# Mixture of experts: weights as one stream, bias products behind the previous gemm, and three smaller edits

## The chip, the cores and the metric

The kernel runs on one core of a Trainium2 chip. The metric is the device time of one execution in microseconds (us), the median of several runs. The engines of the core work in parallel, each with a queue of its own that is worked off in order: TensorE (PE for its products, PEld for its weight loads), VectorE (DVE), ScalarE (ACT), GpSimd (POOL) and SyncE (SP, which issues most DMAs here). An instruction at the head of a queue that waits for a semaphore holds up all that stands behind it on that engine.

## The reference, cut to what matters

Three transformer blocks in sequence, 512 tokens of 1024 features. The change lies in the second half of the first block, a mixture of 32 experts of which each token takes four (two small edits lie in block 1's start and in block 2):

```python
def moe(h, w_router, b_router, w1, b1, w2, b2):       # 512 x 1024
    logits = xf @ w_router + b_router
    top_val, top_idx = lax.top_k(logits, 4)
    gates = jax.nn.softmax(top_val, axis=-1)
    ...                                                # tokens sorted by expert
        u = xb @ w1[e] + b1[e]                         # 1024 -> 2048
        glu = jnp.minimum(u[:, ::2], 7.0)
        lin = jnp.clip(u[:, 1::2], -7.0, 7.0)
        a = glu * jax.nn.sigmoid(1.702 * glu) * (lin + 1.0)
        return a @ w2[e] + b2[e]                       # 1024 -> 1024
    ...                                                # y[token] += gate * result
```

Block 2 is an attention with a scalar `lam`, worked out from four vectors of 64 (`lambda_vecs`), and other mixers.

## The kernel before, in words

`moe` (L933) first ranks the experts by how many tokens they have, on the chip: expert 0 stands at position 0, the others at positions 1 to 31 by falling count. Each position has a block of fixed room: 128 tokens for positions 0 to 5, 96 for 6 to 9, 80 for 10 to 16, 64 for 17 to 31; positions 1 and 2 have a second block of 64 ("heavy"). Positions 3 to 16 are called large, 17 to 31 small. What doesn't fit goes to overflow blocks in a loop at the end (L1416), which runs zero times with these inputs. The order in which the experts are worked is 0, 3, 17, 4, 5, 18, 6, 7, 19, ... : mostly two large ones and a small one, with a heavy one in between and three small ones behind it; the last one is small.

Each expert has three gemms of eight k-tiles: two halves of w1 and then w2. Its weights come in 12 loads of 1 MB on SP's queue (`wload`, L944), into nine buffers `mraw` and two `raw`, one load for two k-tiles. In position order 0 to 16 each k-tile of weights is split into two numbers of reduced precision: ACT writes hi (L302), and DVE lo = raw - hi (L303; POOL for a few tiles of expert 0). The tiles whi/wlo have three buffers, a pair `ws` is used for every fourth. A large expert takes per k-tile six products of 512 columns (hi by x hi, hi by x lo, lo by x hi, two halves each), a small one two, with the raw weights (L1269). The products of one gemm add up in a PSUM bank; large ones alternate between mm0 and mm1, small ones between s0 and s1. Each gemm begins with the bias, itself a product (L1252 for a small block, L1255 for a large one), which opens the bank.

After a w1 half the epilogue reads the bank: DVE gl (L1283), ACT gt (L1284), DVE ln (L1285), DVE twice (L1286, L1287), then PE transposes gl (L1212), and ACT and DVE put the result down as the operand of w2 (L1204, L1206). After w2, `scatter` (L1328) weighs the rows by their gates on ACT (yr, L1330 or L1333) and POOL adds them to `yd` in DRAM by an indirect DMA. Slots without a token are added to 128 extra rows of yd (`dump`).

The tokens of a block come by an indirect DMA of POOL from `hrow`, the normalized tokens in DRAM (L1222, L1226), and are transposed on PE (L1212). For expert 0, four products of 0/1 matrices A0 with the token numbers (L1064) give the list gi. Its first four k-tiles are split ahead (L1180 to L1182): three behind `last`, the operation that writes gi, the fourth with its lo on POOL. The tables of all other blocks (`tables`, L1087, and `tables2`, L1161) are worked out during expert 0.

The order of the instructions in each engine's queue isn't the order of the program alone: a planner draws it up ahead of time, by program order as priority, with costs of its own for every operation and by when it thinks that the operands are there. `tc.issue_after(x)` holds what is inside it behind x on the same engine.

`block2` loads the four vectors (lv, L1515) on POOL's queue and works out the lambdas with a few small operations of DVE and ACT (to L1526).

Of the kernel before, what the change touches and what calls it, by code (L numbers as in the profile page):

```python
# [11 lines left out]
F32 = mybir.dt.float32  # L12
# [10 lines left out]
T = 512  # L23
# [511 lines left out]

def block1_mixer(k):
# [18 lines left out]
    cs = k.silu_col(k.v("c"))  # L555
    b = k.v("b_ada")
# [341 lines left out]
def moe_rows(k):  # L898

    nc = k.nc  # L900
    ps = k.pt("t")[0:8, 0:128]
    nc.tensor.transpose(ps, k.mod1[:, 24:32], k.ident)
    t = k.sm.tile([128, T], F32, tag="tmp", name="sh", bufs=3)
    nc.scalar.activation(t[0:8, 0:128], ps, AF.Copy)
    shd = k.dr.tile([1, D], F32, name="shd")
    nc.gpsimd.dma_start(shd.rearrange("o (n c) -> (o n) c", c=128), t[0:8, 0:128])
    k.hrow = k.dr.tile([T, D], F32, name="hrow")
    nc.gpsimd.dma_start(k.hrow, shd.to_broadcast([T, D]))

    k.yd = k.dr.tile([T + 128, D], F32, name="yd")  # L910
    z = k.sm.tile([128, T], F32, tag="tmp", name="z", bufs=3)
    nc.gpsimd.memset(z, 0.0)
    for j in range(T // 128 + 1):
        nc.gpsimd.dma_start(k.yd[128 * j:128 * j + 128].rearrange("p (a f) -> p a f", a=2), z.unsqueeze(1).to_broadcast([128, 2, T]))
# [18 lines left out]
def moe(k):  # L933
# [42 lines left out]
    gi0 = mp.tile([128, 1], I32, name="gi0")  # L976
# [56 lines left out]
    dump = rp.tile([128, 2], F32, name="dump")  # L1033
    G.tensor_scalar(dump[:, 0:1], pid, T + 1.0, None, op0=ALU.add)
    G.tensor_sub(dump[:, 1:2], pid, half)
    G.tensor_scalar(dump[:, 1:2], dump[:, 1:2], 2.0 * T, None, op0=ALU.add)
# [24 lines left out]
    g0 = pg[:, 128:192]  # L1061
# [20 lines left out]
    V.tensor_tensor(sel[:, :, 0:32], rk[:, 64:96].unsqueeze(1).to_broadcast([128, 2, 32]),  # L1082
# [4 lines left out]
    def tables():  # L1087
# [64 lines left out]
        V.tensor_scalar(pad, tp3[:, 0], 0.5, dump[:, 0:1], op0=ALU.is_lt, op1=ALU.mult)  # L1152
# [4 lines left out]
        V.tensor_scalar(pad[:, c64], tab[:, 0, c64], 0.5, dump[:, 1:2], op0=ALU.is_lt, op1=ALU.mult)  # L1157
# [25 lines left out]
    nsp = [0]  # L1183

    def wsplit(raw, pool_lo, to):
# [3 lines left out]
        return k.wsplit(raw, pool_lo=pool_lo, to=to)  # L1189

# [23 lines left out]

    def gather(blocks):
# [17 lines left out]
    def expert(w1, w2, blocks, selcol, between=None, on_pool=((),) * 3, last=False, to=lambda: None):  # L1233


        X = gather(blocks)
# [7 lines left out]
        def gemm(w, ops, bcol):  # L1244

            pss = []
            for ns, *_ in blocks:
                ps = bank("s").unsqueeze(1) if ns == 64 else bank("mm", (128, 2, 512))
                o = [ps[64 * c:64 * c + 64, 0] if ns == 64 else ps[0:ns, c] for c in range(2)]
                b_ = bias[:, bcol // 2:bcol // 2 + 512]  # L1250
                if ns == 64:
                    nc.tensor.matmul(ps[:, 0], sw, b_, start=True, stop=False)  # L1252
                else:
                    for c in range(2):
                        nc.tensor.matmul(o[c], selcol[:, c].to_broadcast([128, ns]), b_, start=True, stop=False)  # L1255
                pss.append((ps, o))
            for q in range(4):
                raw = w[q]() if callable(w[q]) else w[q]
                for j in range(2):
                    kt = 2 * q + j  # L1260
                    if between and not last and bcol == 1024 and kt == 4:
                        between[0]()
                    if split:
                        hi, lo = ready.pop(0) if ready else wsplit(raw[:, j], kt in on_pool[bcol // 1024], to())
                    for op_, (_, o) in zip(ops, pss):
                        terms = ((op_[0], hi), (op_[0], lo), (op_[1], hi)) if len(op_) == 2 else ((op_[0], raw[:, j]),)
                        for n_, (l, r_) in enumerate(terms):
                            for c in range(2):
                                ins = nc.tensor.matmul(o[c], l(kt), r_[:, c * 512:(c + 1) * 512], start=False,  # L1269
                                                       stop=kt == 7 and n_ == len(terms) - 1)  # L1270
                    if kt == 3:
                        turn["half"] = ins.ins
                    for _ in range(2 if kt > 3 else 0):
                        if adds:
                            adds.pop(0)()
            return [ps if b_[0] == 64 else ps[0:b_[0]] for (ps, _), b_ in zip(pss, blocks)]
        for hf in range(2):
            for ps, (a_, _), (ns, *_) in zip(gemm([w1(hf, q) for q in range(4)], X, hf * 1024), A, blocks):
# [15 lines left out]
        pys = gemm([w2(q) for q in range(4)], [a_[1] for a_ in A], 2048)  # L1294
# [12 lines left out]
    def block(b):  # L1307
        return (ROOM + (64,) * N2)[b], tabi[:, b:b + 1] if b else gi0, tab[:, 0, b:b + 1], tab[:, 1, b:b + 1], tabi[:, b:b + 1]
# [17 lines left out]
    def scatter(py, gcol, row, ns):  # L1326

        y = pools["Y"].tile([128, D], F32, tag="Y", name="yr", bufs=1) if ns == 64 else ep.tile([128, D], F32, tag="ah", name="yr", bufs=2)  # L1328
        if ns == 64:
            S.activation(y[:, 0:512], py[:, 0], AF.Copy, scale=gcol)  # L1330
            G.indirect_dma_start(yd2, IOA(ap=row, axis=0), y[:, 0:512], None, bounds_check=2 * T + 127, compute_op=ALU.add)
# [68 lines left out]
    def first_weights():  # L1400
        w = a["w2_qk"]
        k.pre = {(id(w), u): k.wunit(w, u) for u in range(3)}
    for p in order:
        blocks = [block(p)] + ([block(31 + p)] if 1 <= p <= N2 else [])
        if p == 0:
            expert(lambda hf, q: first[4 * hf + q], lambda q: (lambda: wload(a["w2"][0, q])), blocks, sel[:, :, 0:1], (tables, tables2), ((6,), (2, 4, 6), (3,)))
            continue
        e = nc.values_load(sigi[0:1, p:p + 1], engines=(mybir.EngineType.SP,), min_val=0, max_val=31)
        own = p == order[-1]
        if own:  # L1410
            collected.extend(collect())
        expert(lambda hf, q: (lambda: wload(sq(a["w1"][bass.ds(e, 1), hf, q]), own)),
               lambda q: (lambda: wload(sq(a["w2"][bass.ds(e, 1), q]), own)), blocks, sel[:, :, p:p + 1], last=own,
               between=first_weights if own else None)
    nov = nc.values_load(ovi[0:1, 0:1], min_val=0, max_val=15)
    with tc.For_i(0, nov, 1) as i:  # L1416
# [7 lines left out]
        expert(lambda hf, q: (lambda: wload(sq(a["w1"][bass.ds(e, 1), hf, q]), True)),  # L1424
               lambda q: (lambda: wload(sq(a["w2"][bass.ds(e, 1), q]), True)), [(128, gi, gc[:, 0:1], gc[:, 1:2])], sc, last=True,
               to=lambda: [t_[:, j] for t_ in (mr.tile([128, 2, 1024], F32R, tag="mraw", name="ms", bufs=9),) for j in range(2)])
# [53 lines left out]
def block2(k):  # L1480
# [29 lines left out]
    with ExitStack() as es2:  # L1510
        p = es2.enter_context(tc.tile_pool(name="da", bufs=1))
        eb_ = p.tile([128, T], F32, name="epb")

        lv = p.tile([128, 256], F32, name="lv")
        G.dma_start(lv, a["lamv"].to_broadcast([128, 256]))  # L1515
        lt = p.tile([128, 2, 64], F32, name="lt")
        lvv = lv.rearrange("p (a b d) -> p a b d", a=2, b=2)
        V.tensor_mul(lt, lvv[:, :, 0], lvv[:, :, 1])
        lam = p.tile([128, 4], F32, name="lam")
        V.tensor_reduce(lam[:, 0:2], lt, axis=AX.X, op=ALU.add)  # L1520
        k.ln_exp(k.hi_ins)
        with tc.issue_after(k.tables.ins):
            S.activation(lam[:, 0:2], lam[:, 0:2], AF.Exp)
        V.tensor_sub(lam[:, 2:3], lam[:, 1:2], lam[:, 0:1])
        lam_init = 0.8 - 0.6 * math.exp(-0.3 * 0)
        V.tensor_scalar(lam[:, 3:4], lam[:, 2:3], -lam_init, None, op0=ALU.add)  # L1526
# [784 lines left out]
```

## Time and profile before

| | us |
|---|---|
| median of 3 runs | 3394.36 (3390.3 to 3399.63) |
| profiled execution | 3392.58 |
| its span | 3389.1, with 3.5 around it |
| PE busy in the span | 3209.7 (95%) |
| DVE, ACT, POOL busy | 1923.5, 1339.0, 415.5 |
| the experts in the span | some 711 to 1910 |

Times in the rows are us from the span's start, durations us unless ns is written. L1252 is line 1252 of the kernel. An entry [0.95 <-DVE ln L1285] says that the engine stood idle for 0.95 us before the instruction and that the end of DVE's ln released it. PEclk is the granted clock of TensorE as a share of full speed; the DMA share is the mean busy share of the core's 16 DMA engines. Products on PE are pipelined, so records of one stretch overlap.

### The profile page before, as it was taken

The numbers are of one execution on the slowest core, as the hardware profiler recorded it, in microseconds if no ns is written. First come the engines' busy times: TensorE is split into PE (matmuls) and PEld (weight loads), VectorE is DVE, ScalarE is ACT, GpSimd is POOL, SyncE is SP. The second block draws the span as 40 slices with busy tenths as digits, with TensorE's granted clock in tenths as the row PEclk, the third lists the DMA queues.
The fourth block names the chain that finished last, engine by engine and source line by source line (L and its number), as shares of the span: only waits on it lengthen the run. The fifth ranks groups of instructions, "written<-read, shape, count | busy, mean of one in ns | idle before, by whom it ended". The sixth has DMA issues, their size and how long they took to land. (4 is left out here: it accounts for less than half of the span.)

```text
span 3389.1 us, 41014 instructions
## 1 busy us (share of the span) xinstructions
PE 3209.7 (95%) x15609; PEld 2225.9 (66%) x15609; DVE 1923.5 (57%) x2927; ACT 1339.0 (40%) x1966; POOL 415.5 (12%) x519
## 2 busy tenths in 40 slices
PE   6999999979999999999998799999999999999998
PEld 5778887756755445544342377777776777678887
DVE  7651235467785567754141377766547765555655
ACT  2232344335665456543141245322235433343433
POOL 1223000131000000000100110211121011010001
PEclk9999999989999999999999899999999999999999
DMA  7437323559999999997979521454422210022222
GB/s 265 167 126 235 106 75 119 183 165 346 396 396 368 379 363 350 372 377 270 361 299 359 212 81 51 170 173 169 153 102 91 98 37 3 14 99 87 100 88 86
DMA packets 110680, 668.48 MB, mean 197 GB/s; under 512 B 14416, under 2 KB 14520, under 8 KB 42000
## 3 DMA queue, kind: packets, MB, share of 16 engines
q1 hardware_dynamic: 81952, 573.35, 44.1%
q0 software_dynamic: 28528, 92.48, 9.5%
q8 instruction: 124, 2.03, 0.2%
q14 instruction: 76, 0.62, 0.1%
HBM read 647.56 MB, written 28.63 MB: 200 GB/s over the span
## 5 line engine op out<-in xcount | busy, mean ns | idle before, releaser
L302 ACT ACTIVATE whi<-raw 128x1024 fp32r<-128x1024 f32 x354 | 373.8, 1059 | 661.1 <-PE mm L353 497.5
L303 DVE TENSOR_TENSOR wlo<-raw,whi 128x1024 fp32r<-128x1024 f32 x352 | 435.2, 1239 | 312.2 <-ACT whi L302 305.4
L352 PE MATMUL mm<-h_hi,whi 128*128 128x512 f32 x1440 | 576.7, 400 | 4.6 <-DVE th L637 1.6
L353 PE MATMUL mm<-h_lo,whi 128*128 128x512 f32 x1440 | 576.3, 400 | 0.0
L354 PE MATMUL mm<-h_hi,wlo 128*128 128x512 f32 x1440 | 575.5, 400 | 0.0
L303 DVE TENSOR_TENSOR wlo<-mraw,whi 128x1024 fp32r<-128x1024 f32 x246 | 295.3, 1218 | 75.0 <-ACT whi L302 73.0
L352 PEld LDWEIGHTS mm<-h_hi,whi 128*128 128x128 f32 x1440 | 270.8, 188 | 82.4 <-issue 12.4
L353 PEld LDWEIGHTS mm<-h_lo,whi 128*128 128x128 f32 x1440 | 271.0, 188 | 67.7 <-issue 7.0
L354 PEld LDWEIGHTS mm<-h_hi,wlo 128*128 128x128 f32 x1440 | 271.0, 188 | 67.0 <-issue 5.6
L302 ACT ACTIVATE whi<-mraw 128x1024 fp32r<-128x1024 f32 x248 | 258.6, 1056 | 92.2 <-PE mm L1269 73.7
L1269 PE MATMUL s<-mraw,x 128*64 128x512 f32 x896 | 234.8, 606 | 16.0 <-DMA mraw<-in_w_dram 15.9
L1269 PE MATMUL mm<-whi,x 128*80 128x512 f32 (+2 forms) x816 | 245.6, 405 | 2.7 <-ACT whi L302 2.7
L1283 DVE TENSOR_SCALAR gl<-s 128x256 f32<-128x256 f32 x34 | 14.4, 424 | 315.8 <-PE s L1269 315.8
L1269 PEld LDWEIGHTS mm<-whi,x 128*80 128x80 f32 (+2 forms) x816 | 135.8, 169 | 72.9 <-issue 15.7
L1269 PEld LDWEIGHTS s<-mraw,x 128*64 128x64 f32 x896 | 65.9, 138 | 140.2 <-issue 115.4
L1284 ACT ACTIVATE gt<-gl 128x256 f32<-128x256 f32 (+3 forms) x68 | 35.5, 522 | 285.8 <-DVE gl L1283 284.3
L370 PE MATMUL mm<-whi,h_hi 128*128 128x256 f32 x480 | 138.3, 288 | 3.6 <-ACT rv L589 1.9
L1269 PE MATMUL mm<-wlo,x 128*80 128x512 f32 (+2 forms) x408 | 132.8, 407 | 8.4 <-DVE wlo L303 7.2
L352 PE MATMUL mm<-fhi,whi 128*128 128x512 f32 x352 | 139.5, 396 | 0.0
L353 PE MATMUL mm<-flo,whi 128*128 128x512 f32 x352 | 139.3, 396 | 0.0
L354 PE MATMUL mm<-fhi,wlo 128*128 128x512 f32 x352 | 139.2, 395 | 0.0
L371 PE MATMUL mm<-wlo,h_hi 128*128 128x256 f32 x480 | 136.0, 283 | 2.1 <-DVE wlo L303 2.0
(733 smaller groups left out, 5546.9 us busy)
## 6 DMA issues: line engine op xcount, KB each, us to landing
mraw<-in_w_dram SPq DMA_DIRECT2D x316, 1024.0 KB, 7.8
raw<-in_w_dram SPq DMA_DIRECT2D x68, 1024.0 KB, 7.8
mw<-in_wmod_dram POOLq DMA_DIRECT2D x48, 512.0 KB, 4.3
raw<-in_w_dn_dram SPq DMA_DIRECT2D x24, 1024.0 KB, 4.8
raw<-in_w_gu_dram SPq DMA_DIRECT2D x22, 1024.0 KB, 5.6
raw<-in_w_up_dram SPq DMA_DIRECT2D x22, 1024.0 KB, 4.8
mw<-in_wada_dram POOLq DMA_DIRECT2D x32, 512.0 KB, 4.6
raw<-in_w_aqk_dram SPq DMA_DIRECT2D x12, 1024.0 KB, 4.9
```

Source lines behind the costliest of these rows:

```text
L302: nc.scalar.activation(hi, raw, AF.Copy)
L303: ins = (nc.gpsimd if pool_lo else nc.vector).tensor_sub(lo, raw, hi.bitcast(F32))
L352: nc.tensor.matmul(pss[t], hi[:, k, s], xs[0][:, k0 + k], start=first, stop=False)
L353: nc.tensor.matmul(pss[t], hi[:, k, s], xs[1][:, k0 + k], start=False, stop=False)
L354: nc.tensor.matmul(pss[t], lo[:, k, s], xs[0][:, k0 + k], start=False, stop=last)
L370: nc.tensor.matmul(ps, xs[0][:, k, s], hi[:, k % 4], start=k == 0, stop=False)
L371: nc.tensor.matmul(ps, xs[0][:, k, s], lo[:, k % 4], start=False, stop=False)
L1269: ins = nc.tensor.matmul(o[c], l(kt), r_[:, c * 512:(c + 1) * 512], start=False, stop=kt == 7 and n_ == len(terms) - 1)
L1283: V.tensor_scalar(gl, pg, 7.0, None, op0=ALU.min)
L1284: S.activation(th, gl, AF.Tanh, scale=0.5 * 1.702)
```

## The change

The weights of all experts become one `Stream` of k-tiles. After each k-tile's products it emits the splits of the next three k-tiles (the next six in a small expert), with at most three splits waiting: that is in the program before the epilogue of the gemm at hand, across gemms and experts. The first two splits of expert 0 are emitted before the router, two more behind `last`, which is now the operation that writes `sel` (L1082); POOL takes lo of the k-tiles 6, 10, 12, 14 and 19 of expert 0, as before, but no longer that of 3. The number of an expert is read by SP at its first load.

The bias products of a gemm are held behind the last weights product of the gemm before.

Expert 0's tokens are picked by products (`pick`): the four tiles of tokens stay in SBUF as rows (two in xgs, two in one mraw buffer), and 32 products of a 128x128 piece of them with A0 give x already transposed; ACT and DVE add the shift and split it. The products L1064, gi, the gather and the transposes of expert 0 fall away.

Slots without a token get an index out of bounds, which the indirect DMA skips; yd has 512 rows, and one of five DMAs that zero it falls away. The lambdas of block 2 (`lambdas`, the same operations with the product on POOL) are worked out at the start of block 1 and not at that of block 2. The loop for overflow blocks uses a stream of its own without splits ahead.

```diff
@@ in moe(), before the router
+    early = [k.wsplit(first[0][:, j]) for j in range(2)]
-    rows = [k.wp.tile([128, D], F32, tag="wlo", name="row", bufs=3) for j in range(2)]
-    for t, row in enumerate(xgs + rows):
+    rows = mr.tile([128, 2, 1024], F32, tag="mraw", name="rows", bufs=9)
+    rows = xgs + [rows[:, 0], rows[:, 1]]
+    for t, row in enumerate(rows):
@@ expert 0's places
     for t in range(4):
         V.tensor_scalar(A0[:, t], iota, p0[:, t:t + 1], M[:, 0, t:t + 1], op0=ALU.is_equal, op1=ALU.mult)
-        nc.tensor.matmul(g0, A0[:, t], tok[:, t:t + 1].to_broadcast([128, 64]), start=t == 0, stop=t == 3)
-    V.tensor_scalar(p0[:, 0:1], g0[:, 0:1], 0.5, 100000.0, op0=ALU.is_lt, op1=ALU.mult)
-    last = V.scalar_tensor_tensor(gi0, g0[:, 0:1], -1.0, p0[:, 0:1], op0=ALU.add, op1=ALU.add)
@@
-    V.tensor_tensor(sel[:, :, 0:32], rk[:, 64:96].unsqueeze(1).to_broadcast([128, 2, 32]),
+    last = V.tensor_tensor(sel[:, :, 0:32], rk[:, 64:96].unsqueeze(1).to_broadcast([128, 2, 32]),
@@ tables()
-        V.tensor_scalar(pad, tp3[:, 0], 0.5, dump[:, 0:1], op0=ALU.is_lt, op1=ALU.mult)
+        V.tensor_scalar(pad, tp3[:, 0], 0.5, 100000.0, op0=ALU.is_lt, op1=ALU.mult)
@@
-    with tc.issue_after(last.ins):
-        ready = [k.wsplit(first[j // 2][:, j % 2]) for j in range(3)]
-    ready.append(k.wsplit(first[1][:, 1], True, [ep.tile([128, D], F32R, tag=tag, name="ws", bufs=1) for tag in ("vh", "vl")]))
+    class Stream:
+        def raw(self, u):
+            while len(self.raws) <= u // 2:
+                n = len(self.raws)
+                self.raws.append(self.src[n]())
+            return self.raws[u // 2][:, u % 2]
+        def ahead(self, upto, limit=3):
+            for u in range(self.at, min(upto, len(self.big))):
+                if self.big[u] and u not in self.split:
+                    if len(self.split) >= limit:
+                        return
+                    self.split[u] = wsplit(self.raw(u), u in (6, 10, 12, 14, 19))
+        def take(self):
+            u = self.at
+            if self.big[u]:
+                self.ahead(u + 1, 99)
+            self.at += 1
+            return self.split.pop(u) if self.big[u] else self.raw(u)
...
+    def pick(At):
+        hl, at = operand("x", True, lambda v, kt: v[:, kt])
+        for n in range(8):
+            if n % 4 == 0:
+                ps = k.pt("t").rearrange("p (j s) -> p j s", s=128)
+            for t in range(4):
+                nc.tensor.matmul(ps[:, n % 4], rows[t][:, n * 128:(n + 1) * 128], At[:, t], start=t == 0, stop=t == 3)
+            sh = mod[:, 24 + n:25 + n]
+            S.activation(hl[0][:, n], ps[:, n % 4], AF.Identity, bias=sh)
+            V.scalar_tensor_tensor(hl[1][:, n], ps[:, n % 4], sh, hl[0][:, n].bitcast(F32), op0=ALU.add, op1=ALU.subtract)
+        return [at]
@@ gemm()
-            for ns, *_ in blocks:
-                ps = bank("s").unsqueeze(1) if ns == 64 else bank("mm", (128, 2, 512))
...
+            with tc.issue_after(turn["mm_ins"]) if turn.get("mm_ins") else nullcontext():
+                for ns, *_ in blocks:
...
+            for kt in range(8):
+                w = stream.take()
+                hi, lo = w if split else (None, None)
+                raw = stream.raw(stream.at - 1)
...
+                if not looped:
+                    stream.ahead(stream.at + (3 if split else 6))
+                turn["mm_ins"] = ins.ins
@@ scatter(), alike for both kinds
-            G.indirect_dma_start(yd, IOA(ap=row[0:ns], axis=0), y[0:ns], None, bounds_check=T + 127, compute_op=ALU.add)
+            G.indirect_dma_start(yd, IOA(ap=row[0:ns], axis=0), y[0:ns], None, bounds_check=T - 1, oob_is_err=False, compute_op=ALU.add)
@@ the order loop
+    for p in order:
+        stream.add(p < N1, loads(p, p == order[-1]))
+    stream.split.update(enumerate(early))
+    with tc.issue_after(last.ins):
+        stream.ahead(4, 4)
...
-            expert(lambda hf, q: first[4 * hf + q], ..., blocks, sel[:, :, 0:1], (tables, tables2), ((6,), (2, 4, 6), (3,)))
+            expert(blocks, sel[:, :, 0:1], pick(A0), (tables, tables2))
```

## Rows read from the trace of the kernel before

**Rows 1.** the page, part 1: busy us (share of the span) x instructions, by engine.

```profile
PE 3209.7 (95%) x15609; PEld 2225.9 (66%) x15609; DVE 1923.5 (57%) x2927; ACT 1339.0 (40%) x1966; POOL 415.5 (12%) x519
```

**Rows 2.** waits of PE, 780 to 1860 us: who, for whom, us in total, times, longest.

```profile
PE s L1252 <- DVE ln L1285: 19.8, 21, 1.0
PE s L1252 <- ACT yr L1330: 8.7, 11, 0.8
PE mm L1255 <- ACT yr L1333: 8.6, 11, 0.9
PE mm L1269 <- DVE wlo L303: 7.6, 28, 0.6
PE mm L1269 <- ACT whi L302: 2.7, 6, 0.4
```

**Rows 3.** stretches: us, busy us (x) of PE, PEld, DVE, ACT, POOL, PEclk, DMA share, GB/s.

```profile
1237.20:1267.10 29.90, 26.76 (x113) 8.68 (x113) 4.11 (x11) 4.50 (x10) 4.07 (x5) 1.00 1.00 386
1160.20:1267.10 106.90, 100.39 (x439) 53.96 (x439) 71.40 (x81) 58.51 (x69) 7.96 (x8) 1.00 0.97 371
1140.00:1160.00 20.00, 18.02 (x78) 5.87 (x76) 2.49 (x6) 3.44 (x7) 1.61 (x3) 1.00 1.01 418
1622.00:1707.00 85.00, 79.65 (x338) 26.56 (x336) 10.93 (x26) 10.88 (x23) 13.02 (x13) 1.00 1.01 395
1053.00:1055.00 2.00, 2.00 (x6) 1.34 (x5) 2.00 (x3) 1.93 (x3) 0.00 (x0) 0.52 1.03 430
```

**Rows 4.** a small expert's boundary: start, us, engine, operation, [idle before <-releaser].

```profile
1029.90 0.47 PE L1252 MATMUL s<-bias,sw 128*128 128x512 f32 x1 [0.95 <-DVE ln L1285]
...
1030.37 0.43 DVE L1287 SCALAR_TENSOR_TENSOR gl<-ln,gl 128x256 f32<-128x256 f32 x1
...
1031.31 0.44 PE L1212 MATMUL t<-ident,gl 128*128 128x128 f32 x2
```

**Rows 5.** timeline at the turn from a small expert to a large one.

```profile
1049.55 0.69 ACT L1330 ACTIVATE yr<-s,tab 128x512 f32<-128x512 f32 x1 [4.77 <-PE s L1269]
...
1050.29 0.50 PE L1252 MATMUL s<-bias,sw 128*128 128x512 f32 x1 [0.79 <-ACT yr L1330]
...
1051.24 0.71 PE L1269 MATMUL mm<-whi,x 128*96 128x512 f32 x2 [0.44 <-ACT whi L302]
```

**Rows 6.** timeline of ACT inside a small expert, two splits of the next large one.

```profile
830.05 2.00 ACT L302 ACTIVATE whi<-raw 128x1024 fp32r<-128x1024 f32 x2 [2.15 <-DMA raw<-in_w_dram]
```

**Rows 7.** groups by line, large expert: count | busy us, mean ns | idle.

```profile
L303 DVE TENSOR_TENSOR wlo<-mraw,whi 128x1024 fp32r<-128x1024 f32 x14 | 16.7, 1216 | 0.2 <-ACT whi L302 0.2
```

**Rows 8.** start: timeline of router and expert 0; block 2: L1548; two stretches.

```profile
704.53 0.17 DVE L1071 SCALAR_TENSOR_TENSOR q<-s,ion 128x32 f32<-128x32 f32 x1
704.60 2.67 POOL L303 TENSOR_TENSOR ws<-mraw,ws 128x1024 fp32r<-128x1024 f32 x1
704.74 2.57 DVE L1073 TENSOR_SCALAR cm<-q,kc 32x32 f32<-32x32 f32 x1
...
707.52 1.09 DVE L1063 TENSOR_SCALAR h<-mcst,p,h 128x128 f32<-128x128 f32 x4
...
723.90 1.97 PE L1212 MATMUL t<-ident,xg 128*128 128x128 f32 x8 [10.91 <-DMA xg<-hrow,gi]
725.76 1.22 PE L1269 MATMUL mm<-whi,x 128*128 128x512 f32 x2
...
1984.62 0.83 PE L1548 MATMUL o<-pts,vt 128*128 128x128 f32 x6
...
710.00:725.80 15.80, 4.42 (x16) 3.02 (x15) 7.30 (x31) 0.60 (x1) 4.00 (x3) 0.50 0.61 191
725.80:780.00 54.20, 44.62 (x194) 36.03 (x194) 49.99 (x70) 27.44 (x29) 17.50 (x7) 0.91 0.55 202
```

**Rows 9.** the last expert on PE, and the branch of the overflow loop (ns min/median/max).

```profile
1873.09 6.79 PE L1269 MATMUL s<-mraw,x 128*64 128x512 f32 x16 [13.30 <-DMA mraw<-in_w_dram]
...
L1416 PEldq COMPARE_BRANCH  x3: 101/193/3313, 1927.0 to 1932.2; - x3
```

More of the change, by code (lines that the diff above doesn't have):

```diff
@@ L1 @@
 import math
[L2 removed]
+from contextlib import ExitStack, nullcontext
 import numpy as np
@@ L555, in block1_mixer @@
     cs = k.silu_col(k.v("c"))
+    lambdas(k)
     b = k.v("b_ada")
@@ L1242, in expert, with gemm @@
             G.tensor_copy(sw.rearrange("p (c s) -> p c s", c=2), selcol.to_broadcast([128, 2, 64]))
-        def gemm(w, ops, bcol):
+        def gemm(ops, bcol):
             pss = []
-            for ns, *_ in blocks:
-                ps = bank("s").unsqueeze(1) if ns == 64 else bank("mm", (128, 2, 512))
[L1249 to L1275, printed above, removed]
@@ new lines, in gemm @@
+            with tc.issue_after(turn["mm_ins"]) if turn.get("mm_ins") else nullcontext():
+                for ns, *_ in blocks:
+                    ps = bank("s").unsqueeze(1) if ns == 64 else bank("mm", (128, 2, 512))
+                    o = [ps[64 * c:64 * c + 64, 0] if ns == 64 else ps[0:ns, c] for c in range(2)]
+                    b_ = bias[:, bcol // 2:bcol // 2 + 512]
+                    if ns == 64:
+                        nc.tensor.matmul(ps[:, 0], sw, b_, start=True, stop=False)
+                    else:
+                        for c in range(2):
+                            nc.tensor.matmul(o[c], selcol[:, c].to_broadcast([128, ns]), b_, start=True, stop=False)
+                    pss.append((ps, o))
@@ new lines, in gemm @@
+            for kt in range(8):
+                if between and not last and bcol == 1024 and kt == 4:
+                    between[0]()
+                w = stream.take()
+                hi, lo = w if split else (None, None)
+                raw = stream.raw(stream.at - 1)
+                for op_, (_, o) in zip(ops, pss):
+                    terms = ((op_[0], hi), (op_[0], lo), (op_[1], hi)) if len(op_) == 2 else ((op_[0], raw),)
+                    for n_, (l, r_) in enumerate(terms):
+                        for c in range(2):
+                            ins = nc.tensor.matmul(o[c], l(kt), r_[:, c * 512:(c + 1) * 512], start=False,
+                                                   stop=kt == 7 and n_ == len(terms) - 1)
+                if not looped:
+                    stream.ahead(stream.at + (3 if split else 6))
+                turn["mm_ins"] = ins.ins
+                if kt == 3:
+                    turn["half"] = ins.ins
+                for _ in range(2 if kt > 3 else 0):
+                    if adds:
+                        adds.pop(0)()
@@ L1293, in expert @@
         collected.clear()
-        pys = gemm([w2(q) for q in range(4)], [a_[1] for a_ in A], 2048)
+        pys = gemm([a_[1] for a_ in A], 2048)
         for py, (ns, _, tok, gcol, *row) in zip(pys, blocks):
@@ L1402, in first_weights, with loads, load @@
         k.pre = {(id(w), u): k.wunit(w, u) for u in range(3)}
+    def loads(p, own):
+        if p == 0:
+            return [lambda f=f: f for f in first] + [lambda q=q: wload(a["w2"][0, q]) for q in range(4)]
+        e = []
+        def load(w, *at):
+            if not e:
+                e.append(nc.values_load(sigi[0:1, p:p + 1], engines=(mybir.EngineType.SP,), min_val=0, max_val=31))
+            return wload(sq(a[w][(bass.ds(e[0], 1),) + at]), own)
+        return [lambda hf=hf, q=q: load("w1", hf, q) for hf in range(2) for q in range(4)] + [lambda q=q: load("w2", q) for q in range(4)]
+    for p in order:
+        stream.add(p < N1, loads(p, p == order[-1]))
+    looped = False
+    stream.split.update(enumerate(early))
+    with tc.issue_after(last.ins):
+        stream.ahead(4, 4)
     for p in order:
@@ L1411, in moe @@
             collected.extend(collect())
-        expert(lambda hf, q: (lambda: wload(sq(a["w1"][bass.ds(e, 1), hf, q]), own)),
-               lambda q: (lambda: wload(sq(a["w2"][bass.ds(e, 1), q]), own)), blocks, sel[:, :, p:p + 1], last=own,
-               between=first_weights if own else None)
+        expert(blocks, sel[:, :, p:p + 1], last=own, between=first_weights if own else None)
     nov = nc.values_load(ovi[0:1, 0:1], min_val=0, max_val=15)
```

71 lines of the change are left out of this document (37 added, 34 removed).

## The prediction

> **What bounds the kernel now.** I read the busy line of the page first: PE is busy 95% of the span [rows 1], so what can be won is PE's idle time, a slower clock, or PE work left out. The stretch that the change rewrites is the experts', 711 to 1910 us of the span. The waits of PE over 780 to 1860 us come next: five kinds, 47.4 us together [rows 2]. The reader is to see there that only the last two (10.3 us) are waits for split weights; 37.1 us are waits of the bias products (L1252, L1255) for the engine that empties their PSUM bank. The table by stretches then says whether PE or the DMA queues set the pace [rows 3]: over one period of two large experts and a small one (106.9 us) PE is busy 100.39, the DMA engines 0.97 of the time; in the middle of a small expert the weights came at 418 GB/s over 20 us. At 371 GB/s the period's 39.7 MB would need 39.7/0.418 = 95 us. So PE binds by some 5 us a period, except in three small experts in a row, where PE is busy 79.65 of 85 us and the DMA share is 1.01: there the loads bind as well.
>
> **Part 1, bias products in order.** A bias product of before is issued as soon as the previous gemm has left PE, for a bank that ACT or DVE is still reading, and PE's queue stands behind it. Afterwards it stands behind the last weights product of the gemm before its own, when its bank has long been read.
> - L1255 behind yr: 11 waits, 8.6 us. Nothing else holds PE there: all 8.6 go.
> - L1252 behind ln: 21 waits, 19.8 us. At the boundary of 1028.95 us [rows 4] the bias product waited 0.95 us for ln; weights products followed, and at 1031.31 the transposes of gl, which DVE had finished at 1030.80. If PE goes straight to the weights products it reaches the transposes 1.9 us after the boundary instead of 2.36, and gl is ready 1.85 after it: 0.43 to 0.5 us is won if the transposes keep their place, all 0.95 if they stand later. Bounds 21 x 0.43 = 9.0 and 19.8. I take 9.0, the row's own order.
> - L1252 behind yr: 11 waits, 8.7 us, behind a small expert; [rows 5] show the turn to a large one. There ACT takes yr first and the first split of the large expert behind it, and the first product waits for that split another 0.44 us. Six of the 11 are like this, with the 0.44 behind them; at the other five nothing else holds PE. If the split stays behind yr, PE only reaches it earlier and waits longer, and 5 x 0.79 = 4.0 us are won; if it goes ahead, all 8.7. ACT is idle for 4.77 us before yr there, and at 830 us ACT did take two splits ahead of time [rows 6]. I take 6.
>
> Sum of part 1: 8.6 + 9.0 + 6 = 23.6 us (bounds 21.6 and 37.1).
>
> **Part 2, the splits ahead of the epilogue.** Their number stays the same, 1.22 us each on DVE [rows 7] and no more on ACT; they only move in front of the epilogue. Waits for splits are 10.3 us [rows 2]. Three sets of split buffers and every fourth set beside them allow about three splits ahead, with the change and without it, so only the order can help: I take a third, 3.4 us (bounds 0 and 10.3). What is queued behind a split is the epilogue on DVE, and behind that the transposes on PE: that is the rival on the other side below. SP's loads keep their order and start at most three k-tiles (4 us of PE) sooner.
>
> **Part 3, the first expert's tokens.** Before, PE stands 10.91 us for the gather, transposes eight times from 723.90 and does the first weights product at 725.76 [rows 8]. Afterwards, 32 products of 128x128 with 128 columns, 64 records, follow A0, whose last row DVE finishes at 708.6. Six such records that followed each other took 0.83 us at full clock, some 0.14 each [rows 8]: 9 us; at the half clock granted in this stretch (0.50), 18 us. ACT and DVE read them while they run; after the last of a kind about 0.5 us. First weights product: 718 to 727. I take 720, nearer to the full clock since the products run in a row there, a gain of 6; it is worth less where expert 0 is then held by DVE, which is busy 49.99 of its 54.20 us [rows 8]. Bounds: -2 (half clock all along) and +10 (full clock, and 2.4 us less on DVE by the split below). The split that leaves POOL takes 2.67 us there, and a DVE operation of 32x32 beside it took 2.57 us, where one of 128x32 just before took 0.17 [rows 8]; if that goes too it is in the upper bound.
>
> **Part 4, what costs nothing.** The rows of empty slots no longer go to yd, one of the five zeroing DMAs and the few dump operations on POOL fall away: POOL is busy 12% and nobody waits for those DMAs in [rows 2]: 0 (bounds -1 and +2, if the transfers are cheaper for the weights' loads in the triples). The lambdas of block 2: what PE stands for ahead of it is the overflow loop's end, one branch of 3.31 us [rows 9], and the lambdas are needed later; so 0 (bounds -1 and +2), and at the start of block 1 a handful of DVE and ACT operations and one load on POOL's queue, which the modulation's loads follow: 0 (bounds -2 and 0). The last expert's 13.30 us for its weights [rows 9] stays: its loads stand on SP behind those of block 2, and this order isn't touched.
>
> **The sum.** 23.6 + 3.4 + 6 = 33.0 us off the profiled execution's 3392.6 (its span of 3389.1 and 3.5 around it), 3359.6. The median of the runs lies 1.8 us above that execution, so 3361 for the median. Own range of this case, with the bounds of the parts but not all of them at once: 3345 to 3374.
>
> **A rule against it.** Over the period the weights come at 371 GB/s and in one stretch at 418 [rows 3]. The Trainium skill (SBUF — State Buffer, "A bandwidth-pool intuition that's wrong (but worth ruling out)") gives the path from HBM to a NeuronCore about 358 GB/s and calls HBM almost always the bottleneck; by that figure the period's 39.7 MB would need an estimated 111 us, more than the 106.9 measured, and nothing could be won in the steady stretch. The trace disagrees, and I give the rule's consequence only the chance of the second rival.
>
> A second one bears on the split that leaves POOL. Under the 2.67 us split on POOL, DVE's small operation was stretched from 0.17 to 2.57 us [rows 8]. The Trainium skill (SBUF — State Buffer, "Who interferes with whom") says that DVE and GpSimd share a port pair by an exclusive lock, held for the whole instruction, which agrees; by it the router's chain would end 2.4 us sooner and part 3 would give 8.4 instead of 6.
>
> **The rivals.**
> - *All the idle time goes.* The transposes fall behind more products, the splits are always there: 47.4 us of [rows 2] instead of 27.0, and three stretches of half clock behind the stalls, as at 1053 to 1055 us [rows 3], where 2.00 us at 0.52 cost 1.0, go too: 20.4 + 3 more, 3338. For it: behind the heavy experts and at 830 [rows 6] work ahead is possible; against it: the transposes' place and the DMA share of 0.97.
> - *The loads bind.* What PE no longer waits for a bank it waits for a load; only the start's 6 us stay: 3388. For it: shares 0.97 to 1.01 [rows 3]. Against it: no wait for a load is among [rows 2].
> - *It moves nothing.* The order in each engine's queue is drawn from estimated costs; the splits come out where they stood, the waits of the bias products turn into waits for gl at the transposes and for split weights, and the start gains nothing: 3393.
> - *Slower: splits in front of the epilogue.* If DVE takes one more split (1.22 us) before gl and ln at both w1 boundaries of the 16 larger experts behind the first, and the transposes keep their place in PE's queue, PE waits 32 x 1.22 = 39 us, and with the start's gain lost too it ends at 3361 + 39 + 6 = 3406. It decides from 33/32, about one split a boundary, on; less than one and the forecast only shrinks. For it: DVE is busy 71.40 of 106.9 us and nearly all of that lies in the two large experts [rows 3]. Against it: only three sets of buffers, so that the third split ahead must wait for PE to leave one, which is nearly the end of the gemm.
>
> **How the numbers follow.** Forecast 0.48, all idle time 0.20, loads bind 0.07, nothing 0.11, slower 0.14. 0.3% is about what a measurement here can tell from no change, 10 us: faster below 3384, slower above 3404.5. Faster is 0.48 + 0.20 and a little of the second rival: 0.70; same 0.16; slower 0.14. The range goes from 3326 (below the first rival by the rest of the clock's and the start's bounds) to 3395 (the third): it leaves out part of the first rival and the whole fourth, some 0.2.
>
> **What would show it.** Right: in the waits of PE the three bias rows are gone or under 3 us, and t L1212 behind gl stands in their place with about 11 us; the first weights product comes at 718 to 723 us; the period of [rows 3] is down by 2 to 3 us. Wrong: waits for mraw loads in the steady stretch (second rival), waits of the transposes for gl of over 1 us in the large experts (fourth), a start later than 726, or a last expert that no longer waits 13 us for its loads.

## The result, and the profile after

The changed kernel takes 3357.87 us (median of four runs, 3355.98 to 3360.36) against 3392.33 before: ratio 0.989, 95% interval 0.986 to 0.992. The forecast was 3361, with a range of its own from 3345 to 3374. The profiled execution took 3355.98 us, its span is 3354.2. The busy line of the page after, beside [rows 1]:

```profile
PE 3210.9 (96%) x15657; PEld 2236.1 (67%) x15657; DVE 1920.1 (57%) x2931; ACT 1337.2 (40%) x1972; POOL 411.0 (12%) x514
```

PE's busy time is all but the same (3210.9 against 3209.7 us); its idle time in the span fell from 179.4 to 143.3 us. To see where, the spans are cut at products that both kernels have: the router's first count product (L1050 before, L1066 after), the first weights product of an expert (L1269, L1321), block 2's first product after the experts (L1502, L1574). Read from the start times in the traces of the profiled executions, in us:

| stretch | before | after | difference |
|---|---|---|---|
| span's start to the router | 703.5 | 700.3 | -3.3 |
| router to expert 3 | 77.7 | 64.1 | -13.6 |
| experts 3, 17, 4, 5, 18 | 162.5 | 165.8 | +3.3 |
| experts 6 to 16 with their small ones | 579.7 | 560.7 | -19.0 |
| experts 24 to 30 | 349.8 | 341.3 | -8.5 |
| the last expert, and to block 2 | 59.4 | 59.4 | 0.0 |
| the rest | 1456.6 | 1462.7 | +6.1 |

The line of experts 24 to 30 holds the two heavy ones as well. The first line is the clock: ahead of the router the granted clock stood at 0.5 for 10.2 us before and for 3.4 after, and the router came at 696.9 to 705.2 us in the kernels below whose code is the changed one's up to there. In the last line some 3 of the 6.1 us are the clock (29.8 us at half clock before, 35.9 after); the other 3 go with the lambdas (e11). The waits of PE after, from expert 3 to the first product of expert 31 (who, for whom, us in total, times, longest), beside [rows 2]:

```profile
PE t L1252 <- DVE gl L1342: 10.6, 20, 0.6
PE s L1321 <- ACT x L1244: 9.8, 10, 1.3
PE mm L1321 <- ACT whi L302: 6.7, 6, 1.1
PE mm L1321 <- DVE wlo L303: 4.3, 10, 0.6
PE mm L1321 <- ACT a L1244: 1.8, 3, 0.6
```

The three bias rows, 37.1 us, are gone. In their place stand the wait of the transposes for gl, 10.6 us, which the prediction had named, and one it had not: 9.8 us for x, at the first product of a small expert. The waits for whi have grown from 2.7 to 6.7, those for wlo have fallen from 7.6 to 4.3. All waits together fell from 47.4 to 33.1 us, 14.3 of the 24.1 us that the experts won. The stretches of the table, the third one only to the first product of expert 30, before and after (columns as in [rows 3]):

```profile
781.20:943.70 162.50, 160.27 (x716) 105.29 (x715) 109.49 (x124) 92.25 (x105) 18.39 (x14) 1.00 1.00 384
943.70:1523.30 579.60, 545.35 (x2357) 303.59 (x2357) 392.09 (x434) 319.99 (x369) 41.86 (x37) 0.99 0.98 371
1523.30:1831.07 307.77, 297.06 (x1185) 118.34 (x1184) 97.99 (x136) 80.99 (x110) 29.03 (x28) 1.00 0.84 325
```

```profile
764.40:930.20 165.80, 162.86 (x714) 104.79 (x712) 109.78 (x124) 92.10 (x106) 17.63 (x14) 1.00 0.99 379
930.20:1490.80 560.60, 536.64 (x2356) 306.87 (x2356) 392.75 (x434) 318.14 (x369) 41.56 (x37) 0.99 0.98 380
1490.80:1793.03 302.23, 296.20 (x1189) 118.85 (x1189) 97.98 (x136) 80.36 (x110) 28.08 (x27) 1.00 0.84 328
```

In the middle stretch PE's busy time fell by 8.7 us with the same number of products. Short stalls show in no wait and stand in the busy time, as a later start of the next record: from a whi product to the wlo product behind it the starts lie more than 0.27 us apart, without idle time between them, in 25 places before and in 10 after, together 6.6 and 2.4 us beyond the 0.233 of an unhindered one. So the waits that the table counts were not the whole of what could be won. These places go with the splits ahead: there are 24 in e1 and in e4 and 26 in e2, which have none, and 11 in e3, which has them.

### The profile page after: what moved, and what is told of

Its sections match the earlier page's. It is cut to its first block, busy times and chain, and to the rows that moved or that the text cites. A ratio compares the mean times of both kernels' runs of the same rounds, so it can differ in the third digit from the quotient of the medians.

```text
span 3354.2 us, 41112 instructions
## 1 busy us (share of the span) xinstructions
PE 3210.9 (96%) x15657; PEld 2236.1 (67%) x15657; DVE 1920.1 (57%) x2931; ACT 1337.2 (40%) x1972; POOL 411.0 (12%) x514
## 5 line engine op out<-in xcount | busy, mean ns | idle before, releaser
L1321 PE MATMUL s<-mraw,x 128*64 128x512 f32 x896 | 235.4, 605 | 23.9 <-DMA mraw<-in_w_dram 15.5
L1321 PE MATMUL mm<-whi,x 128*80 128x512 f32 (+2 forms) x816 | 242.4, 403 | 6.7 <-ACT whi L302 6.7
L1321 PEld LDWEIGHTS mm<-whi,x 128*80 128x80 f32 (+2 forms) x816 | 134.6, 168 | 76.2 <-issue 13.5
L1321 PEld LDWEIGHTS s<-mraw,x 128*64 128x64 f32 x896 | 65.7, 138 | 146.4 <-issue 123.3
L1321 PE MATMUL mm<-wlo,x 128*80 128x512 f32 (+2 forms) x408 | 131.7, 404 | 5.6 <-DVE wlo L303 4.3
```

## The experiments

All stretches are read as in the table above: *start* is router to expert 3, *experts* is expert 3 to 31 (1091.9 before, 1067.8 after). *Half* counts the stretches of half clock in the experts, 3.4 us each, without the one in which PE waits for the last expert's loads. At half the speed such a stretch costs an estimated 1.7 us, and *level* is *experts* less 1.7 us for each. How many there are differs between kernels with the same stalls (last section), so gains are compared by *level*. Each row of stretches is one execution.

| kernel | start | first five | 6 to 16 | 24 to 30 | experts | half | level | median us | ratio, 95% |
|---|---|---|---|---|---|---|---|---|---|
| before | 77.7 | 162.5 | 579.7 | 349.8 | 1091.9 | 3 | 1086.8 | | |
| changed | 64.1 | 165.8 | 560.7 | 341.3 | 1067.8 | 3 | 1062.7 | 3357.87 | 0.989 (0.986 to 0.992) |
| e1 | 76.8 | 161.9 | 571.4 | 342.5 | 1075.8 | 1 | 1074.1 | 3373.79 | 0.9943 (0.9923 to 0.9963) |
| e2 | 67.0 | 163.6 | 581.0 | 348.7 | 1093.3 | 4 | 1086.5 | 3383.33 | 0.9966 (0.9952 to 0.9981) |
| e3 | 67.4 | 166.4 | 566.8 | 347.7 | 1080.8 | 4 | 1074.0 | 3374.17 | 0.9949 (0.9931 to 0.9968) |
| e4 | 62.8 | 162.8 | 571.2 | 341.5 | 1075.5 | 1 | 1073.8 | 3364.32 | 0.9926 (0.9901 to 0.9951) |
| e5 | 64.8 | 166.9 | 562.2 | 343.5 | 1072.6 | 4 | 1065.8 | 3353.87 | 0.9875 (0.9856 to 0.9894) |
| e6 | 62.9 | 165.8 | 560.6 | 329.1 | 1055.5 | 3 | 1050.4 | 3347.09 | 0.986 (0.9842 to 0.9878) |
| e7 | 64.5 | 165.6 | 549.1 | 339.0 | 1053.7 | 1 | 1052.0 | 3345.86 | 0.9854 (0.9835 to 0.9872) |
| e8 | 63.9 | 164.6 | 544.4 | 341.3 | 1050.3 | 0 | 1050.3 | 3342.84 | 0.9846 (0.9829 to 0.9863) |
| e9 | 63.0 | 164.6 | 535.9 | 326.2 | 1026.7 | 0 | 1026.7 | 3323.32 | 0.9791 (0.9774 to 0.9807) |
| e10 | 61.9 | 161.5 | 535.9 | 326.2 | 1023.7 | 0 | 1023.7 | 3314.34 | 0.9782 (0.9755 to 0.981) |
| e11 | 62.0 | 162.5 | 536.1 | 326.2 | 1024.8 | 0 | 1024.8 | 3312.8 | 0.9775 (0.9758 to 0.9793) |

**e1, the order of the bias products alone** (on the kernel before):

```diff
+            with tc.issue_after(turn["mm_ins"]) if turn.get("mm_ins") else nullcontext():
                 for ns, *_ in blocks:
...
+                    turn["mm_ins"] = ins.ins
...
```

> The kernel before with one edit: the bias products are held behind the last weights product of the gemm before. Theory A (the bias products carry the steady gain): the three bias rows vanish from PE's waits, transposes wait for gl some 10 us instead, and first weights product of expert 3 to that of expert 31 shortens by 18 to 24 us (changed kernel: 1067.8 against 1091.9, so 24.1 less): about 3372. Theory B (the bias products only clear the way, the splits ahead carry it): under 8 us, about 3386, with the waits moved to whi and wlo.

The experts are 16.1 us shorter, but one stretch of half clock falls into them where there were three: by level it is 12.7 us, between the two theories. Waits of PE in e1, expert 3 to the first product of expert 31:

```profile
PE t L1212 <- DVE gl L1289: 11.4, 22, 0.6
PE s L1270 <- ACT x L1204: 8.5, 10, 1.1
PE mm L1270 <- DVE wlo L303: 7.7, 28, 0.6
PE mm L1270 <- ACT whi L302: 6.7, 6, 1.1
PE mm L1270 <- ACT x L1204: 2.8, 5, 0.6
```

Without the splits ahead waits for gl, x and whi appear as in the changed kernel: they come of the order of the bias products. All waits together are 37.0 us, 10.4 less than before.

**e2, the first expert's tokens alone** (on the kernel before): `pick(A0)` and the rows kept in SBUF.

> The kernel before with expert 0's tokens picked by products, nothing else. Theory A (the start is a part of its own): expert 3 begins 9 to 14 us earlier and the lead stays: about 3381. Theory B (the loads take it back in the first experts, where the DMA share is 0.97 to 1.02): the lead is down to under 5 us by expert 6: about 3388.

The start is 10.6 us shorter, and the lead is 9.5 us at expert 6 and 9.3 at expert 31: theory A. One us of it is lost again by expert 6; no wait for a load stands among PE's waits there, and why is open. By level the experts take as long as before (1086.5 for 1086.8).

**e3, the changed kernel with early bias products:**

```diff
-            with tc.issue_after(turn["mm_ins"]) if turn.get("mm_ins") else nullcontext():
+            with nullcontext():
```

> The changed kernel with its bias products free to be issued early again. Theory A: the bias rows are back with 30 us or more, the steady part loses 15 to 24 us of its 24.1, the start's lead stays: about 3375. Theory B: the splits ahead keep most of it: under 3365.

Waits of PE in e3, expert 3 to 31, the five largest:

```profile
PE s L1306 <- DVE ln L1340: 19.9, 21, 1.0
PE s L1306 <- ACT yr L1385: 8.7, 11, 0.8
PE mm L1309 <- ACT yr L1388: 6.5, 6, 1.1
PE mm L1321 <- DVE wlo L303: 4.3, 10, 0.6
PE mm L1321 <- ACT whi L302: 2.7, 6, 0.4
```

The rows of the bias products are back, 35.1 us. The experts lose 13.1 of their 24.1 us (11.3 by level), under theory A's range. Against e2, which has neither edit, the experts of e3 are 12.5 us shorter; both had four stretches of half clock. That is the splits ahead, with the new scatter.

**e4, the changed kernel without splits ahead in the gemms:**

```diff
-                if not looped:
-                    stream.ahead(stream.at + (3 if split else 6))
```

> The changed kernel without the splits ahead: each is emitted at its own k-tile, as before the change. Theory A (they give little, and in the first large experts they put the epilogue late): PE's waits for a (1.8 us) and the extra 1.2 us of each of the first three large experts go, waits for whi and wlo come back to about 10 us: 3355 to 3365. Theory B (they carry the steady gain): 3375 or more.

Neither theory holds whole. The median lies in theory A's range, PE's waits for a are gone and the first five experts are 3.0 us shorter, but the middle is 10.5 us longer, so the splits ahead do not give little. The experts lose 7.8 us in all, and 11.1 by level, since e4 had one stretch of half clock for three. By level the two edits add: the bias products win 12.7 us alone and the splits ahead 11.1 on top of them, or the splits 12.5 and the bias products 11.3, of the 24.1 in all.

**e5, the old scatter and the old lambdas** put back into the changed kernel (640 rows of yd with `dump`, the lambdas at block 2's start).

> The changed kernel with two of its edits taken back: the rows of empty slots are added to 128 extra rows again (with the fifth zeroing DMA), and the lambdas are worked out at the start of block 2 again. Theory A (both are worth nothing): the steady part (expert 3 to expert 31) within 1.5 us of 1067.8, from the end of the experts to the middle of block 2 within 1 us, the whole within its uncertainty of 3358. Theory B (the fewer rows relieve the weights' loads where these bind): the steady part 4 us or more longer, 3363.

The median does not get worse (3353.87). The experts are 4.9 us longer, which is neither theory's reading as it stands: four stretches of half clock fell into them where the changed kernel had three (1.7 us), and the last expert's wait for its loads is 14.3 us and not 12.0. What is left, 0.9 us, these two traces can't tell apart.

**e6, the last expert's loads first** (on the changed kernel; `own_load` lists the loads of weights in their order):

```diff
+        with tc.issue_after(own_load[-5].ins):
             k.pre = {(id(w), u): k.wunit(w, u) for u in range(3)}
```

> The changed kernel with block 2's prefetch held, on SP, behind the eighth load of the last expert. Theory A (the last expert waits because its loads stand behind that prefetch): its 12 us wait for the loads goes, block 2 begins 8 to 12 us sooner: about 3348. Theory B (the loads come late for another reason, their buffers, or block 2 then waits for its own weights): under 3 us, 3356.

SP's queue in the changed kernel, PE behind it, and SP's queue in e6:

```profile
1823.75 0.33 SPq L296 DMA_DIRECT2D raw<-in_w_v_dram  x1
1824.28 25.75 SPq L969 DMA_DIRECT2D mraw<-in_w_dram  x12
```

```profile
1832.11 6.46 PE L1321 MATMUL s<-mraw,x 128*64 128x512 f32 x16 [12.04 <-DMA mraw<-in_w_dram]
```

```profile
1791.57 36.70 SPq L969 DMA_DIRECT2D mraw<-in_w_dram  x13
1828.32 0.90 SPq L296 DMA_DIRECT2D raw<-in_w_qk_dram  x2
```

Behind block 2's loads the last expert's first load went out at 1824.28; ahead of them its twelve, with the load before them, went out from 1791.57 on, PE no longer stands for them, and from the router to block 2 the kernel takes 10.7 us less (1180.6 for 1191.3). Theory A.

**e7, the next expert's tokens early** (on the changed kernel; `nxt` holds the blocks of the next expert):

```diff
+        if nxt:
+            turn["X"] = gather(nxt)
         pys = gemm([a_[1] for a_ in A], 2048)
...
```

> The changed kernel with the next expert's tokens gathered and transposed ahead of w2 of the expert at hand. Theory A (PE's wait for x at a small expert's first product, 9.8 us in 10 waits, is ACT taking yr before x): that row goes, 6 to 9 us less in the steady part: about 3350. Theory B (the wait moves to yr, the gather or the split): under 3 us: 3356.

Waits of PE in e7, expert 3 to 31:

```profile
PE t L1252 <- DVE gl L1342: 10.5, 20, 0.6
PE mm L1321 <- ACT whi L302: 6.6, 6, 1.1
PE mm L1321 <- DVE wlo L303: 4.3, 10, 0.6
PE mm L1321 <- ACT a L1244: 1.8, 3, 0.6
```

The wait for x is gone, the experts are 14.0 us shorter, more than the 9.8 us of the wait: one stretch of half clock falls into them where there were three, and by level it is 10.7 us. Theory A.

**e8, splits ahead of yr** (on the changed kernel; `whi_ins` is the last write of a hi by then):

```diff
+            with tc.issue_after(k.whi_ins.ins):
                 S.activation(y[:, 0:512], py[:, 0], AF.Copy, scale=gcol)
```

> The changed kernel with yr of a 64-row block held behind the splits already taken ahead, on ACT. Theory A (the first product of a large expert behind a small one waits for a split only because ACT takes yr first): the wait for whi, 6.7 us in 6, and part of that for wlo go, and the half clock behind them: 6 to 10 us, about 3350. Theory B (the weights have not landed by then): yr comes later and PE waits for whi as long as before: 3358 or more.

Waits of PE in e8, expert 3 to 31:

```profile
PE t L1252 <- DVE gl L1342: 10.5, 20, 0.6
PE s L1321 <- ACT x L1244: 9.8, 10, 1.3
PE mm L1321 <- ACT a L1244: 1.8, 3, 0.6
PE mm L1321 <- DVE wlo L303: 0.9, 4, 0.2
```

The wait for whi is gone and wlo is at 0.9: 10.1 us of waits. The three stretches of half clock behind those turns are gone as well (an estimated 5.1 us), and the experts are 17.5 us shorter, well over what was expected: the time at half clock was priced too low. The 2.3 us that are left stand in PE's busy time, which falls from 536.64 to 529.35 us in the middle stretch, 5.1 of it the clock.

**e9, e6 to e8 together.**

> The changed kernel with the three additions of e6, e7 and e8 together. Theory A (they take away three different waits, so their gains add): end of the experts some 8 (tokens) + 17 (splits before yr) + 10 (last loads) = 35 us sooner against the router: about 3358 - 33 = 3325. Theory B (PE then runs into the loads, DMA share 0.98 in the middle third, and the rest turns into waits for weights): 3335 or more.

The experts are 41.0 us shorter than in the changed kernel; e6, e7 and e8 alone gave 12.2, 14.0 and 17.5. e7 and e8 both count stretches of half clock that can go only once; by level it is 12.3, 10.7 and 12.4, 35.4 together, and 36.0 in e9: the gains add, theory A. The rest of its profiled execution holds 31 us of half clock in a row in block 3, which no other has, so it is read by its experts alone.

**e10, no splits ahead inside the experts of 128 rows** (on e9):

```diff
-                if not looped:
+                if not looped and not (split and blocks[0][0] == 128):
                     stream.ahead(stream.at + (3 if split else 6))
```

> e9, with no splits emitted ahead inside the experts of 128 rows (positions 0 to 5). Theory A (in these the splits ahead put the epilogue, and with it the operand of w2, late): experts 3, 4 and 5 take some 36.3 us each and not 37.4 to 38.0, PE's wait for a goes: 3 to 4 us less than e9. Theory B (the 1.2 us are the price of something else of the stream): no difference, or the experts behind them start with waits for whi: 0 to 3 us more.

Waits of PE in e10, expert 3 to 31:

```profile
PE t L1253 <- DVE gl L1343: 11.0, 21, 0.6
PE mm L1322 <- DVE wlo L303: 0.9, 4, 0.2
```

The first five experts are 3.1 us shorter, the others as in e9, and the wait for a is gone: theory A. The intervals of the two kernels' ratios overlap; the stretch shows it, the times alone don't.

**e11, e10 with the lambdas in block 2 again.**

> e10 with the lambdas worked out at the start of block 2 again, nothing else. From block 2's first product of the normed rows (L1591 of the changed kernel) to the end, the kernels with the lambdas there took 1456.6 to 1461.0 us in their profiles, those with the lambdas moved 1461.2 to 1465.5. Theory A (moving them costs 2 to 3 us behind that point, spread over blocks 2 and 3): block 2 to the end of the attention part 143.0 to 143.6 and the next long stretch 453.1 to 453.3, not 143.7 to 144.1 and 453.8 to 454.0: about 3312. Theory B (those differences come from the scatter or from the clock): as in e10, 3314.

(The line meant is L1574.) Theory A's two stretches read 143.3 and 453.5 for e10's 143.8 and 453.9. From that product to the end e11 takes 1461.4 us and e10 1462.4, with 38.0 and 35.7 us at half clock; less half of that time, an estimate of what the clock costs, it is 1442.4 and 1444.6: 2.2 us. Read in this way the five kernels with the lambdas in block 2 (before, e1, e2, e5, e11) take 1441.7 to 1442.4 us there, and seven of the eight with the lambdas moved 1444.4 to 1445.7 (e9, with its 84 us of half clock, 1441.5). So moving them costs 2 to 3 us: theory A, though its second stretch fell by 0.4 only. The medians, 3312.8 and 3314.34, can't tell e11 from e10; its experts are 1.1 us longer with nothing changed in them, so about one us between two traces says nothing.

## Why the prediction was right, point by point

The mechanism was right in the main: what went is time in which PE stood at the boundaries and at the start, and the loads did not take it back. That the sum came so near (34.5 us between the medians, 33.0 forecast) is luck. In the profiled executions the experts gave 24.1 us where 27.0 had been added up, the start 13.6 and not 6, the clock ahead of the router 3.3, and block 2 and behind took 6.1 back. Inside the experts the two terms were off by 11 and 8 us in opposite directions. Of the signs named, the bias rows are gone, gl stands with 10.6 us for about 11, the period of [rows 3] takes 104.8 us for 106.9, and the last expert still waits; only the first weights product, at 707.6 us, lies outside its 718 to 723.

**Bias products: 23.6 forecast, 12.7 by level alone (16.1 as measured) and 11.3 beside the other edits (13.1).** The step that failed is "Nothing else holds PE there: all 8.6 go". At the turn from a large expert to a small one, before and after (timelines):

```profile
1020.07 1.11 ACT L1333 ACTIVATE yr<-mm,tab 96x1024 f32<-96x1024 f32 x1 [4.52 <-PE mm L1269]
...
1021.08 0.58 ACT L1204 ACTIVATE x<-t 128x512 f32<-128x512 f32 x1
...
1021.23 0.70 PE L1255 MATMUL mm<-bias,sel 128*96 128x512 f32 x2 [0.87 <-ACT yr L1333]
...
1021.86 0.65 PE L1269 MATMUL s<-mraw,x 128*64 128x512 f32 x2
```

```profile
1003.70 0.48 PE L1306 MATMUL s<-bias,sw 128*128 128x512 f32 x1
1003.87 1.11 ACT L1388 ACTIVATE yr<-mm,tab 96x1024 f32<-96x1024 f32 x1 [3.98 <-PE mm L1321]
...
1004.88 0.58 ACT L1244 ACTIVATE x<-t 128x512 f32<-128x512 f32 x1
...
1005.52 0.65 PE L1321 MATMUL s<-mraw,x 128*64 128x512 f32 x2 [1.34 <-ACT x L1244]
```

Before, PE waited for yr to empty the bank; afterwards the bias product goes at once, and the first weights product waits for x. ACT does x behind yr in both kernels, and from yr's start PE does its first weights product after 1.79 us before and 1.65 after: 0.14 of the 0.87 us is won. Six of the 11 waits are at such a turn; the other five, between two large experts, became waits for x of 0.5 to 0.6 us in e1 and are gone only with the splits ahead. e7, which puts x ahead of yr, is the test. At L1252 behind ln the forecast held: 19.8 us of waits became 10.6 for gl over the same experts, 9.2 less, with 9.0 the lower bound that had been taken. (The 1.9 us in its working don't follow from [rows 4]: 2.36 less the wait of 0.95 is 1.41, and PE then waits some 0.5 us for gl, as it does here.) At L1252 behind yr the split stayed behind yr on ACT at the six turns to a large expert, and the waits for whi grew from 2.7 to 6.7 us: 4.7 of the 8.7 are won, in waits, nearer to the lower bound of 4.0 than to 6; e8 shows what the other order gives.

**Splits ahead: 3.4 forecast, 11.1 by level beside the ordered bias products (e4; 7.8 as measured), 12.5 without them (e3 against e2, the scatter included).** Of the waits it went as forecast: with the splits ahead they are 33.1 us for 36.9 in e4, and those for wlo 4.3 for 7.6. The term was mis-sized since it counted only the waits of [rows 2]: the short stalls that stand in the busy time fell by 4.0 us more (6.4 to 2.4), and some 3 us are not traced to a place. The rival on the other side is in it too, with its mechanism and small: in expert 4 DVE takes splits between the operations of the epilogue, and PE comes to the transposes of gl just before it needs their result (timelines of DVE and of PE):

```profile
854.02 0.69 DVE L1341 SCALAR_TENSOR_TENSOR gl<-gt,gl 128x512 f32<-128x512 f32 x1 [0.23 <-ACT gt L1339]
854.63 1.22 DVE L303 TENSOR_TENSOR wlo<-mraw,whi 128x1024 fp32r<-128x1024 f32 x1
855.77 0.68 DVE L1342 SCALAR_TENSOR_TENSOR gl<-ln,gl 128x512 f32<-128x512 f32 x1
856.37 1.22 DVE L303 TENSOR_TENSOR wlo<-mraw,whi 128x1024 fp32r<-128x1024 f32 x1
```

```profile
856.51 0.66 PE L1252 MATMUL t<-ident,gl 128*128 128x128 f32 x4
...
858.20 0.74 PE L1321 MATMUL mm<-whi,a 128*128 128x512 f32 x2 [0.60 <-ACT a L1244]
```

gl is ready at 856.45, the transposes run at once, and PE stands 0.60 us for a. That is 29.38 us behind the expert's first product; in e10, where one split less stands ahead of the epilogue and none between these two operations, gl is ready after 28.25. Such an expert takes 37.4 to 38.0 us, without the splits ahead 36.3 to 36.9. It happened in the experts of 128 rows only, three of them at one boundary each, and not at 32 boundaries. e10 shows that it comes of the splits ahead in these experts; that it comes by this order on DVE is read from the two timelines. Why the ones of 96 and 80 rows are free of it is open.

**The first expert's tokens: 6 forecast, 10.6 alone, 13.6 in the change, outside the bound of 10.** Start of the changed kernel, PE and then one operation of DVE:

```profile
702.76 1.59 PE L1262 MATMUL t<-h,xg 128*128 128x128 f32 x6
...
707.56 0.69 PE L1321 MATMUL mm<-whi,x 128*128 128x512 f32 x2
...
714.15 0.61 PE L1262 MATMUL t<-h,rows 128*128 128x128 f32 x4
```

```profile
701.47 0.23 DVE L1085 TENSOR_SCALAR cm<-q,kc 32x32 f32<-32x32 f32 x1
```

The step that failed: the forecast let the weights products begin when the picking ends, at 720. They began at 707.56 in between; the last pick products ran at 714.15, with some 0.15 us a record, so the full clock's value held there (the granted clock was 0.5 from 700.9 to 707.7 us and 1 behind it). The 32x32 operation of [rows 8] takes 0.23 us now that POOL's split is away, 2.3 less; in e2, which still has that split, it takes 2.57 us as before. That agrees with the exclusive lock of the Trainium skill (SBUF — State Buffer, "Who interferes with whom"). e2's start of 67.0 us holds that operation; the kernels without it, and with the first splits ahead of the router, take 61.9 to 64.8, but e3 67.4. Half clock of different length lies in these starts, so how the part beyond e2's 10.6 divides is open. What binds next is DVE in expert 0, as the forecast had it (waits of PE, 700 to 780 us, after):

```profile
PE t L1252 <- DVE gl L1342: 5.9, 2, 3.7
...
PE mm L1321 <- POOL wlo L303: 0.6, 1, 0.6
```

**What was put at nothing:** the scatter's 0.9 us (e5) can't be told from nothing. The lambdas cost 2 to 3 us in blocks 2 and 3 (e11), where the bound had been 1: that PE stands for something else at the start of block 2 does not make them free behind it. By which instruction they cost is open. The last expert's wait stayed, 12.0 for 13.30 us, and e6 confirms the reason given.

**The rivals.** The loads do not bind: no load stands among PE's waits between expert 3 and expert 30, the middle stretch went from 371 to 380 GB/s, and e9 takes another 25 us out of it, at 396 GB/s. (The prediction's 95 us a period is worked out at 418 GB/s, and not at the 371 that its sentence names.) The 358 GB/s of the Trainium skill (SBUF — State Buffer, "A bandwidth-pool intuition that's wrong (but worth ruling out)") are passed over 560 us here, with the kernel on one core. That all idle time goes did not come: e7 and e8 were needed for the waits for x and whi and for the half clock, and even e10 keeps 11.0 us of waits for gl.

## What to carry to other kernels

A wait in a table names who came last, not what stands behind: before a wait is booked as a gain, look which operand the next instruction needs and where its producer stands in its engine's queue; here x stood behind yr on ACT, and reordering ACT (e7, e8) gave 14.0 and 17.5 us (10.7 and 12.4 by level) beside the 11.3 of the bias products. Work taken ahead on an engine that also does an epilogue must not be issued ahead of that epilogue or between its operations where the result is needed soon. Cut both traces at the same products, and count the stretches of half clock before two traces are compared: three of the parts here were off by 8 to 11 us and the sum by 1.5, and of e1's 16.1 us 3.4 are the clock.

With e6 to e8 and e10 added to the change the kernel takes 3314.34 us (ratio 0.9782, 0.9755 to 0.981), less than the kernel before and the changed one.

## What the runs showed of the hardware

In the changed kernel PE waits 1.10 us for whi and 0.56 for wlo at each of six turns from a small expert to a large one. Behind three of them (1034, 1140 and 1348 us) the granted clock then fell to 0.5, the lower level of 1.2 GHz, for 3.4 us; behind the others it did not. With the same waits it fell behind four of the six in e5 and behind one in e1, e4 and e7. Such a stretch costs about 1.6 us, as long as the stall itself: expert 14 with one takes 38.84 us from first product to first product, expert 12, of the same room and at the same place of the order, 37.24 without. In e8 to e11 these stalls are gone, and no stretch of half clock falls between expert 3 and the wait for the last expert's loads.
